# Wide projection blocks for the mixed values and the second gate in a two-layer encoder

## The chip, the cores and the metric

The kernel runs on one core of one Trainium2 chip. The metric is device time in microseconds (us) of one launch, from the first instruction to the end; the median of three runs stands for a kernel. All data are float32 in the chip's memory. The engines are PE (matrix products), ACT (activations and copies), DVE (vector work on tiles, also from PSUM), POOL (further vector work) and SP, which here only issues DMAs.

## The reference

Two layers over 2048 tokens of 1024 channels. Each layer normalises its input, projects it once into seven column ranges, and joins two kinds of mixing:

```python
SPLITS = (D_A, D_A, D_A, D_B, D_KV, D_KV, D_B)      # 512 512 512 512 128 128 512
for l in range(DEPTH):
    h = rmsnorm(x, pre_g[l])
    proj = jnp.einsum('bsd,de->bse', h, w_in[l])
    u_a, v_a, g_a, q, k, v, g_b = jnp.split(proj, idx, axis=-1)
    y_a = gmlp_group(u_a, v_a, ln_a_g[l], ln_a_b[l], spatial_w[l], spatial_b[l]) * jax.nn.silu(g_a)
    y_b = gqa_axial_attention(q, k, v, q_norm_g[l], k_norm_g[l], tables) * jax.nn.silu(g_b)
    y = jnp.concatenate([y_a, y_b], axis=-1)
    out = jnp.einsum('bse,ed->bsd', y, w_out[l])
    x = x + rmsnorm(out, post_g[l])
```

gmlp_group normalises the values v_a over their channels and mixes them across each chunk of 128 tokens with a 128x128 matrix per channel group, and adds a bias. gqa_axial_attention normalises and rotates queries (8 heads) and keys (2 heads), and attends over all 2048 tokens.

## The kernel before

*Precision.* Each float32 operand of a projection is split into a high part (hi, rounded to the matrix engine's float32 form) and a low part (lo, what is left). A projection is three passes, PASSES = ((0,0), (0,1), (1,0)), high by high, high by low and low by high, each over ND = 8 slices of 128 input channels: 24 matmuls for one tile of output.

*Tokens.* The 2048 tokens are four groups of 512 (GRP), a group is four tiles of 128 (TPG). A layer first projects everything and then attends. The projection (`run`) goes over two halves of two groups; the normalised, transposed activations of a group are two tiles `hT` (slices 0 to 3 and 4 to 7), which stay in place for all blocks of the half.

*Blocks of a half, in program order.* Weight columns come in blocks of 256 (WB). Keys and values (C_K) and the first half of the queries (C_Q) alternate by group; then the second half of the queries (C_Q+WB) for both groups; then the values of the mixing (C_VA, and C_VA+WB into the other half of the same PSUM bank) for both groups; then the gate of the attention, here called the second gate (C_GB, then C_GB+WB), each for both groups; then four blocks that join 128 columns of the first gate (C_GA) with 128 of u (C_U). In all blocks but the last four the activations are PE's stationary operand and 256 columns of weights move (`proj_tok`, out 128 tokens by 256 columns); two such tiles share one bank (`banked`). In the last four the weights are stationary and 512 tokens move (`proj_ch`). So seven of the blocks are narrow: 256 columns.

*Weights.* `load_w` (L257) brings 1 MB of raw columns by a DMA of SP; `split_w` makes hi on ACT (L267) and lo on DVE (L268) in two instructions each. Raw, hi and lo each take one slot of a pool of seven, 8 KB a partition. A load is recorded where its block is prepared and waits for its slot.

*Work behind a projection.* `do_kv` and `do_q` normalise and rotate (`norm_rope`: ACT squares, DVE reduces at L351, scales at L358, multiplies at L363 and adds at L365; POOL multiplies at L360) and hand transposes to PE for later; the results of the queries go through L411 and to memory. `do_va` takes statistics of four value tiles on DVE, scales them (L429), splits them (ACT L435, POOL L436, tile fl) and mixes: three matmuls of 256 columns per piece, read out by DVE (L448, two instructions a piece, with zbias). `do_gb` is a tanh on ACT, a product on DVE (L476) and a store. `spatial_weights` loads and transposes the mixing matrices (wsT, L233), stores their two parts and works out the bias tile zbias (L250).

*What sets the order.* PE runs in the order of the program. A list of background jobs (`bg`) is called at each `tick`, twice at most, and puts transposes and mixes between the projection's matmuls some ticks after they were asked for. The order of ACT, DVE, POOL and SP in this phase comes from a scheduler that runs before the launch; on the chip each engine takes its instructions strictly in that order. Seven PSUM banks go round among all of it (projections `pp`, transposes and mixes `pt`, maxima `pmax`). In the second half of a layer the maxima of the first attention units already run between the gate blocks.

Of the kernel before, what the change touches and what calls it, by code (L numbers as in the profile page):

```python
# [9 lines left out]
F32 = mybir.dt.float32  # L10
# [3 lines left out]
AF = mybir.ActivationFunctionType  # L14
# [5 lines left out]
P = 128  # L20
# [18 lines left out]
def encoder(ctx: ExitStack, tc, x, w_in, w_out, pre_g, post_g, ln_a_g, ln_a_b,  # L39
# [135 lines left out]
    class Project:  # L175
# [85 lines left out]
        def split_w(self, raw, n=4):  # L261
# [7 lines left out]
            return hi, lo  # L269

        def hT_jobs(self, g, tail=False):

# [41 lines left out]
        def proj_tok(self, hT, j, w, ps=None, c0=0):  # L314
            if ps is None:
                ps = ps_t("pp")
            n = 0
            for a, b in PASSES:
                for d in range(ND):
                    PE.matmul(ps[:, c0:c0 + WB], hT[d // 4][:, a, d % 4, j * P:(j + 1) * P], w[b][:, d, :],  # L320
                              start=(n == 0), stop=(n == 3 * ND - 1))
                    n += 1
                bg.tick()
            return ps

# [145 lines left out]

        def do_gb(self, g, banks, b):
            for i, ps in enumerate(banks):
                th = f_t("fa")
                nc.scalar.activation(th, ps, AF.Tanh, scale=0.5)
                nc.vector.scalar_tensor_tensor(th, th, 1.0, ps, ALU.add, ALU.mult)  # L476
                nc.sync.dma_start(gb_d[g][:, 2 * i:2 * i + 2, b * WB:(b + 1) * WB],
                                  th.rearrange("p (t e) -> p t e", t=2))

# [41 lines left out]
        def run(self, kv, first, last_jobs, first_wo):  # L521
# [5 lines left out]
            for n, gs in enumerate(halves):  # L527
# [13 lines left out]
                for i, g in enumerate(gs):  # L541
# [4 lines left out]
                    if i == len(gs) - 1:  # L546
                        raw = self.load_w([C_Q + WB])
                    self.do_kv(g, self.banked(hTs[g], w_kv))
                    if i == len(gs) - 1:
                        w_next = self.split_w(raw)  # L550
                        raw = self.load_w([C_VA])
                    self.do_q(g, self.banked(hTs[g], w), 0)
                if n == 0:
                    self.spatial_weights()
                w = w_next
                for i, g in enumerate(gs):
                    self.do_q(g, self.banked(hTs[g], w), 1)
                    if i == 0:
                        w_next = self.split_w(raw)
                w = w_next  # L560
                raw = self.load_w([C_VA + WB])
                ws = [row_t("ws", dt=F32R) for _ in range(2)]
                for i in range(2):
                    nc.sync.dma_start(ws[i].bitcast(F32), ws_d[:, i])
                w = [w, self.split_w(raw)]
                raw = self.load_w([C_GB])
                for g in gs:
                    vs = []
                    for j in range(TPG):
                        ps = self.proj_tok(hTs[g], j, w[0])  # L570
                        self.proj_tok(hTs[g], j, w[1], ps, WB)
                        v = f_t("fv")
                        nc.scalar.copy(v, ps)
                        vs.append(v)
                    self.do_va(g, vs, ws)
                w = self.split_w(raw)
                blocks = [[C_GB + WB]] + [[C_GA + c * P, C_U + c * P] for c in range(4)]
                if n + 1 < len(halves):
                    blocks.append([C_K])
                if n + 1 == len(halves):  # L580
                    self.scale_v()
                    last_jobs()
                for b in range(2):
                    raw = self.load_w(blocks.pop(0))
                    for i, g in enumerate(gs):
                        self.do_gb(g, self.banked(hTs[g], w), b)
                        if i == 0:
                            w_next = self.split_w(raw)
                    w = w_next
                for c in range(4):  # L590
# [641 lines left out]
```

## Time and profile before

| what | us |
|---|---|
| median of three runs (2775.23 to 2775.82) | 2775.79 |
| the profiled execution | 2771.47 |
| its span, first to last instruction | 2769.3 |
| PE busy in the span | 2677.1 |
| DVE busy | 1896.8 |
| ACT busy | 1522.7 |
| POOL busy | 1287.0 |

The mean clock that PE was granted was 0.992 of full speed. The rows of the profile in this text have these forms. A group of instructions: line, engine, operation, output<-inputs by their names in the program, shapes, count | busy time of the group, mean duration of one in ns | idle time of the engine just ahead of them and what ended it. A row of the timeline: start, length, engine, line, operation, count, and in brackets the idle time ahead of it with what ended it. A row of the waits: the engine and its line, what it waited for, then the total, the number of times and the longest. A row of a stretch: its start and end, its length, then busy time and count of PE, PE's weight loads, DVE, ACT and POOL, the granted clock, the busy share of the DMA engines, and GB/s.

### The profile page before, as it was taken

The numbers are of one execution on the slowest core, as the hardware profiler recorded it, in microseconds if no ns is written. First come the engines' busy times: TensorE is split into PE (matmuls) and PEld (weight loads), VectorE is DVE, ScalarE is ACT, GpSimd is POOL, SyncE is SP. The second block draws the span as 40 slices with busy tenths as digits, with TensorE's granted clock in tenths as the row PEclk, the third lists the DMA queues.
The fourth block names the chain that finished last, engine by engine and source line by source line (L and its number), as shares of the span: only waits on it lengthen the run. The fifth ranks groups of instructions, "written<-read, shape, count | busy, mean of one in ns | idle before, by whom it ended". The sixth has DMA issues, their size and how long they took to land.

```text
span 2769.3 us, 48428 instructions
## 1 busy us (share of the span) xinstructions
PE 2677.1 (97%) x18230; PEld 1782.0 (64%) x18230; DVE 1896.8 (68%) x3796; ACT 1522.7 (55%) x3005; POOL 1287.0 (46%) x1080
## 2 busy tenths in 40 slices
PE   7999999999999999999999999999999999999997
PEld 6898899764444444444589989997644444444444
DVE  8862688876666776776487528888766666666664
ACT  4221432117887787787732214221288877778774
POOL 1210122007786676776632101210277767667765
PEclk9999999999999999999999999999999999999999
DMA  4424522322222232222354334333322222221313
GB/s 143 146 81 127 165 76 81 112 63 89 89 71 81 75 98 79 82 80 80 110 179 138 115 114 134 88 92 98 94 64 72 82 70 73 81 76 47 112 46 129
DMA packets 275310, 265.31 MB, mean 96 GB/s; under 512 B 19202, under 2 KB 233346, under 8 KB 275076
## 3 DMA queue, kind: packets, MB, share of 16 engines
q1 hardware_dynamic: 275076, 262.22, 30.2%
q8 instruction: 143, 2.34, 0.3%
q14 instruction: 91, 0.75, 0.1%
HBM read 177.09 MB, written 85.07 MB: 95 GB/s over the span
## 4 chain that ended last, share of the span: by engine, by line
PE 77%; DVE 11%; ACT 5%; DMA 3%; issue 2%; POOL 1%; SPq 0%; DVEq 0%; POOLq 0%; ACTq 0%
PE pp L84 27%; PE sp L84 14%; PE po L84 11%; PE pout L84 11%; PE pmax L84 7%; PE sums L84 4%; PE pt L84 2%; DVE fc L363 2%; ACT p_parts L84 2%; ACT p_f L84 2%; DMA w_raw<-in_w_in_dram 1%; DVE mx L84 1%; DVE o_t L84 1%; DVE w_lo L268 1%; ACT w_hi L267 1%
## 5 line engine op out<-in xcount | busy, mean ns | idle before, releaser
L84 POOL TENSOR_TENSOR p_parts<-p_f,p_parts 128x512 f16<-128x512 f32 x872 | 1034.9, 1205 | 404.2 <-ACT p_f L84 304.3
L84 ACT ACTIVATE p_parts<-sp 128x512 f16<-128x512 f32 x1024 | 630.0, 615 | 296.5 <-PE sp L84 289.8
L84 DVE TENSOR_REDUCE mx<-pmax 128x1 f32<-128x512 f32 x768 | 513.0, 681 | 211.9 <-PE pmax L84 209.9
L84 PE MATMUL pout<-wo,y_t 128*128 128x512 f32 x1488 | 657.1, 506 | 0.7 <-ACT p_f L84 0.3
L84 PE MATMUL po<-p_parts,v_st 128*32 128x512 f16 (+1 forms) x3072 | 639.2, 383 | 0.2
L84 ACT ACTIVATE p_f<-sp 128x512 f32<-128x512 f32 x1024 | 632.0, 617 | 0.0
L84 PE MATMUL pp<-w_hi,hT 128*128 128x256 f32 x3584 | 502.5, 290 | 16.1 <-DVE hT L310 9.7
L84 PEld LDWEIGHTS pp<-w_hi,hT 128*128 128x128 f32 x3584 | 462.0, 194 | 21.8 <-DVE hT L310 10.9
L84 PE MATMUL sp<-q_st,k_t 128*128 128x512 f16 x1024 | 390.2, 381 | 8.3 <-DVE mx L84 5.5
L84 PE MATMUL pmax<-k_t,q_m 128*128 128x512 f16 x1024 | 389.7, 382 | 7.6 <-DVE mx L84 3.2
L84 PEld LDWEIGHTS <-v_st 128*32 128x32 f16 (+1 forms) x3072 | 193.7, 96 | 309.5 <-issue 253.0
L84 PE MATMUL sp<-q,k_t 66*128 66x512 f16 x1024 | 391.0, 382 | 0.0
L84 PEld LDWEIGHTS pout<-wo,y_t 128*128 128x128 f32 x1488 | 281.3, 190 | 128.4 <-issue 8.7
L84 PEld LDWEIGHTS <-k_t 128*128 128x128 f16 (+1 forms) x2048 | 191.5, 99 | 187.7 <-issue 74.4
L468 POOL TENSOR_TENSOR fl<-fa,fh 128x512 fp32r<-128x512 f32 x32 | 43.1, 1346 | 533.3 <-ACT fh L467 489.2
L84 PE MATMUL pp<-hT,w_hi 128*128 128x512 f32 x1024 | 271.7, 413 | 0.0
L84 PE MATMUL pp<-w_lo,hT 128*128 128x256 f32 x1792 | 262.6, 290 | 0.0
L84 PE MATMUL sums<-p_parts,one_h 128*32 128x512 f16 x2048 | 242.3, 380 | 0.0
L84 PEld LDWEIGHTS pp<-w_lo,hT 128*128 128x128 f32 x1792 | 235.5, 194 | 0.9
L84 PEld LDWEIGHTS pp<-hT,w_hi 128*128 128x128 f32 x1024 | 193.4, 190 | 35.3
L683 DVE TENSOR_REDUCE mx<-pmax 128x1 f32<-128x512 f32 x256 | 172.6, 687 | 49.1 <-PE pmax L84 47.5
L84 PEld LDWEIGHTS <-q_m 128*128 128x128 f16 x1024 | 99.8, 98 | 140.2 <-issue 42.1
(161 smaller groups left out, 2790.9 us busy)
## 6 DMA issues: line engine op xcount, KB each, us to landing
w_raw<-in_w_in_dram SPq DMA_DIRECT2D x28, 1024.0 KB
y_t<-y_d SPq DMA_DIRECT2D x56, 512.0 KB
w_raw<-in_w_in_dram SPq DMA_DIRECT2D x32, 512.0 KB
x_t<-in_x_dram SPq DMA_DIRECT2D x16, 512.0 KB
z_d<-fb SPq DMA_DIRECT2D x32, 256.0 KB
gb_d<-fa SPq DMA_DIRECT2D x32, 256.0 KB
fb<-z_d SPq DMA_DIRECT2D x32, 256.0 KB
y_d<-fh SPq DMA_DIRECT2D x32, 256.0 KB
```

What stands on the lines that cost most here:

```text
L84: return tc.keep_in_program_order(call(*args, **kw))
L267: nc.scalar.copy(hi[:, sl], raw[:, sl])
L268: nc.vector.tensor_tensor(lo[:, sl], raw[:, sl], hi.bitcast(F32)[:, sl], ALU.subtract)
L363: nc.vector.tensor_tensor(t2[:, :, :, lo:lo + 16], qn[:, :, :, hi:hi + 16], tbi[:, :, 1:2, lo:lo + 16].broadcast_to([P, 2, n, 16]), ALU.mult)
L468: nc.gpsimd.tensor_tensor(lo, th, hi.bitcast(F32), ALU.subtract)
L683: dve.tensor_reduce(s.mx[:, j, c:c + 1], ps, AX.X, ALU.max)
```

## The change

The values of the mixing and the second gate are projected in blocks of 512 columns. A wide block comes as two raws of 1 MB, each 512 columns of four slices of 128 input channels (`load_wide`), and is split into four tiles, hi and lo for slices 0 to 3 and 4 to 7 (`split_wide`); all six take slots of the same pool of seven. `proj_wide` runs the 24 matmuls of a token tile at 512 columns, with the activations stationary, and ticks after every four, so six times a tile, as the two narrow calls did together. `do_gb` now stores whole rows of a token tile. The second half of the queries moves behind the values: the order of a half is keys and first queries by group, values (wide), second queries (narrow), second gate (wide), then the four blocks of first gate and u. `spatial_weights` is called right after the first group's keys, where it came after all keys and first queries.

```diff
+        def load_wide(self, c):
+            raws = [w_t([P, ND // 2, 2 * WB], "w_raw", F32) for _ in range(2)]
+            for q, raw in enumerate(raws):
+                nc.sync.dma_start(raw, w_in[self.l, q * GRP:(q + 1) * GRP, c:c + 2 * WB]
+                                  .rearrange("(d p) e -> p d e", p=P))
+            return raws
+
+        def split_wide(self, raws):
+            parts = [], []
+            for raw in raws:
+                hi, lo = [w_t([P, ND // 2, 2 * WB], name) for name in ("w_hi", "w_lo")]
+                for d in range(0, ND // 2, 2):
+                    sl = slice(d, d + 2)
+                    nc.scalar.copy(hi[:, sl], raw[:, sl])
+                    nc.vector.tensor_tensor(lo[:, sl], raw[:, sl], hi.bitcast(F32)[:, sl], ALU.subtract)
+                parts[0].append(hi)
+                parts[1].append(lo)
+            return parts
...
+        def proj_wide(self, hT, j, w):
+            ps = ps_t("pp")
+            n = 0
+            for a, b in PASSES:
+                for d in range(ND):
+                    PE.matmul(ps, hT[d // 4][:, a, d % 4, j * P:(j + 1) * P], w[b][d // 4][:, d % 4, :],
+                              start=(n == 0), stop=(n == 3 * ND - 1))
+                    n += 1
+                    if n % 4 == 0:
+                        bg.tick()
+            return ps
...
-        def do_gb(self, g, banks, b):
-            for i, ps in enumerate(banks):
-                th = f_t("fa")
-                nc.scalar.activation(th, ps, AF.Tanh, scale=0.5)
-                nc.vector.scalar_tensor_tensor(th, th, 1.0, ps, ALU.add, ALU.mult)
-                nc.sync.dma_start(gb_d[g][:, 2 * i:2 * i + 2, b * WB:(b + 1) * WB],
-                                  th.rearrange("p (t e) -> p t e", t=2))
+        def do_gb(self, g, j, ps):
+            th = f_t("fa")
+            nc.scalar.activation(th, ps, AF.Tanh, scale=0.5)
+            nc.vector.scalar_tensor_tensor(th, th, 1.0, ps, ALU.add, ALU.mult)
+            nc.sync.dma_start(gb_d[g][:, j], th)
...
                     if i == len(gs) - 1:
-                        raw = self.load_w([C_Q + WB])
+                        raws = self.load_wide(C_VA)
                     self.do_kv(g, self.banked(hTs[g], w_kv))
+                    if n == 0 and i == 0:
+                        self.spatial_weights()
                     if i == len(gs) - 1:
-                        w_next = self.split_w(raw)
-                        raw = self.load_w([C_VA])
+                        w_next = self.split_wide(raws)
                     self.do_q(g, self.banked(hTs[g], w), 0)
-                if n == 0:
-                    self.spatial_weights()
                 w = w_next
-                for i, g in enumerate(gs):
-                    self.do_q(g, self.banked(hTs[g], w), 1)
-                    if i == 0:
-                        w_next = self.split_w(raw)
-                w = w_next
-                raw = self.load_w([C_VA + WB])
                 ws = [row_t("ws", dt=F32R) for _ in range(2)]
                 for i in range(2):
                     nc.sync.dma_start(ws[i].bitcast(F32), ws_d[:, i])
-                w = [w, self.split_w(raw)]
-                raw = self.load_w([C_GB])
-                for g in gs:
+                raw = self.load_w([C_Q + WB])
+                for i, g in enumerate(gs):
                     vs = []
                     for j in range(TPG):
-                        ps = self.proj_tok(hTs[g], j, w[0])
-                        self.proj_tok(hTs[g], j, w[1], ps, WB)
+                        ps = self.proj_wide(hTs[g], j, w)
                         v = f_t("fv")
                         nc.scalar.copy(v, ps)
                         vs.append(v)
                     self.do_va(g, vs, ws)
-                w = self.split_w(raw)
-                blocks = [[C_GB + WB]] + [[C_GA + c * P, C_U + c * P] for c in range(4)]
+                    if i == 0:
+                        w_next = self.split_w(raw)
+                w = w_next
+                raws = self.load_wide(C_GB)
+                for i, g in enumerate(gs):
+                    self.do_q(g, self.banked(hTs[g], w), 1)
+                    if i == 0:
+                        w_next = self.split_wide(raws)
+                w = w_next
+                blocks = [[C_GA + c * P, C_U + c * P] for c in range(4)]
...
-                for b in range(2):
-                    raw = self.load_w(blocks.pop(0))
-                    for i, g in enumerate(gs):
-                        self.do_gb(g, self.banked(hTs[g], w), b)
-                        if i == 0:
-                            w_next = self.split_w(raw)
-                    w = w_next
+                raw = self.load_w(blocks.pop(0))
+                for i, g in enumerate(gs):
+                    for j in range(TPG):
+                        self.do_gb(g, j, self.proj_wide(hTs[g], j, w))
+                    if i == 0:
+                        w_next = self.split_w(raw)
+                w = w_next
```

First, PE at the start of the value stage in the first half of layer 0. A row is one or several like instructions, output<-stationary and moving operands in the order of the program's names, the output's shape and a count; numbers tell tiles of one name apart. Before, a value tile begins with the last zbias matmuls (pt from wsT and sb_row) between its passes:

```order
L84 MATMUL pp_1479<-w_hi_1267,hT_145 128x256 x4
L84 MATMUL pp_1479<-w_hi_1267,hT_146 128x256 x4
L84 MATMUL pp_1479<-w_lo_1268,hT_145 128x256 x4
L84 MATMUL pp_1479<-w_lo_1268,hT_146 128x256 x4
L84 MATMUL pt_1496<-wsT_1098,fb_1107 128x256
L84 MATMUL pt_1496<-sb_row_1109,ones1_86 128x256
L84 MATMUL pp_1479<-w_hi_1267,hT_145 128x256 x4
L84 MATMUL pp_1479<-w_hi_1267,hT_146 128x256 x4
L84 MATMUL pp_1479<-w_hi_1471,hT_145 128x256 x4
L84 MATMUL pp_1479<-w_hi_1471,hT_146 128x256 x4
```

And now, at the same place:

```order
L84 MATMUL pp_1163<-w_hi_953,hT_145 128x512 x4
L84 MATMUL pp_1163<-w_hi_959,hT_146 128x512 x4
L84 MATMUL pp_1163<-w_lo_954,hT_145 128x512 x4
L84 MATMUL pp_1163<-w_lo_960,hT_146 128x512 x4
L84 MATMUL pp_1163<-w_hi_953,hT_145 128x512 x4
L84 MATMUL pp_1163<-w_hi_959,hT_146 128x512 x4
L84 MATMUL pp_1190<-w_hi_953,hT_145 128x512 x4
L84 MATMUL pp_1190<-w_hi_959,hT_146 128x512 x4
L84 MATMUL pt_1199<-ident_81,kk_947 128x128 x2
```

A tile is 24 matmuls of 512 columns where two times 24 of 256 stood, from four weight tiles, and the zbias matmuls have moved ahead of the stage.

Second, DVE at the end of the value stage of the same half, where the values of the second group are made ready. Before, their scaling (fv, L429) follows on the statistics, and the split of the weights of the first block of first gate and u (w_lo_2597) stands behind it; fb are mixes of the first group's last tile:

```order
L448 SCALAR_TENSOR_TENSOR fb_2082<-pt_2171,lng_1095,zbias_1097 64x128
L429 TENSOR_SCALAR fv_1843<-fv_1843,mv_v_2091,rs_y_2106 128x512
L429 TENSOR_SCALAR fv_1924<-fv_1924,mv_v_2091,rs_y_2106 128x512
L429 TENSOR_SCALAR fv_2005<-fv_2005,mv_v_2091,rs_y_2106 128x512
L429 TENSOR_SCALAR fv_2089<-fv_2089,mv_v_2091,rs_y_2106 128x512
L268 TENSOR_TENSOR w_lo_2597<-w_raw_2468,w_hi_2596 128x1024 x2
```

And now, with the lines of the changed program (L286 is the subtraction of `split_wide`, L481 the mix, L462 the scaling):

```order
L123 TENSOR_TENSOR rs_t_1579<-rs_y_1578 128x4
L286 TENSOR_TENSOR w_lo_1803<-w_raw_1595,w_hi_1802 128x1024
L124 SCALAR_TENSOR_TENSOR rs_t_1579<-rs_t_1579,ms_v_1564 128x4
L481 SCALAR_TENSOR_TENSOR fb_1554<-pt_1639,lng_552,zbias_554 64x128
L125 SCALAR_TENSOR_TENSOR rs_y_1578<-rs_t_1579,rs_y_1578 128x4
L481 SCALAR_TENSOR_TENSOR fb_1554<-pt_1639,lng_552,zbias_554 64x128
L123 TENSOR_TENSOR rs_t_1579<-rs_y_1578 128x4
L286 TENSOR_TENSOR w_lo_1803<-w_raw_1595,w_hi_1802 128x1024
```

The split of the second gate's second raw (w_raw_1595) now stands within the steps that lead to the scaling, ahead of all four scalings.

Third, SP's issues around that load. Before, two loads of weights of the first gate and u (w_raw) stand among the stores of mixed values (z_d) and of the gate (gb_d):

```order
L452 DMA z_d0_140<-fb_2016 512x1x128
L257 DMA w_raw_2468<-in_w_in_dram 128x8x128 x2
L452 DMA z_d0_140<-fb_2082 512x1x128
L257 DMA w_raw_2708<-in_w_in_dram 128x8x128 x2
L477 DMA gb_d0_120<-fa_2285 128x2x256
```

And now:

```order
L485 DMA z_d0_140<-fb_1455 512x1x128
L275 DMA w_raw_1595<-in_w_in_dram 128x4x512
L485 DMA z_d0_140<-fb_1508 512x1x128
L485 DMA z_d0_140<-fb_1554 512x1x128
L257 DMA w_raw_2012<-in_w_in_dram 128x8x128 x2
L373 DMA fa_1753<-in_rope_dram 128x4x128
```

The wide block's second raw stands ahead of two stores of mixed values, the weights of the first gate and u and a table of rotations (fa from rope) for the queries.

## The prediction, made before the changed kernel ran

> **What bounds the kernel now.** I read the busy shares first, then the chain that ended last, then PE's groups, and last the waits of PE in the stages that the change touches.
>
> ```profile
> PE 2677.1 (97%) x18230; PEld 1782.0 (64%) x18230; DVE 1896.8 (68%) x3796; ACT 1522.7 (55%) x3005; POOL 1287.0 (46%) x1080
> PE 77%; DVE 11%; ACT 5%; DMA 3%; issue 2%; POOL 1%; SPq 0%; DVEq 0%; POOLq 0%; ACTq 0%
> ```
>
> PE is busy for 2677.1 of 2769.3 us, and every other engine is at 68% or less: time goes only where PE issues faster or waits less. Over the whole program PE's rate counts, so the price of one matmul must be right. The groups by shape are the obvious place for it, and they mislead:
>
> ```profile
> L84 PE MATMUL pp<-w_hi,hT 128*128 128x256 f32 x3584 | 502.5, 290 | 16.1 <-DVE hT L310 9.7 <-DVE zbias L250 4.5 <-DVE k_t L396 1.2
> L84 PE MATMUL pp<-hT,w_hi 128*128 128x512 f32 x1024 | 271.7, 413 | 0.0
> ```
>
> 3584 matmuls of 290 ns would be 1039 us, yet the group was busy for 502.5: one matmul is still draining while the next runs, so the mean is no spacing. 2 x 290 - 413 = 167 ns would promise 256 us for the 1536 pairs below, which is wrong. The spacing is read from starts in stretches without a wait:
>
> ```profile
> 208.10 2.08 PE L84 MATMUL pp<-w_hi,hT 128*128 128x256 f32 x16
> 210.03 1.12 PE L84 MATMUL pp<-w_lo,hT 128*128 128x256 f32 x8
> 210.99 2.08 PE L84 MATMUL pp<-w_hi,hT 128*128 128x256 f32 x16
> ...
> 244.50 1.98 PE L84 MATMUL pp<-hT,w_lo 128*128 128x512 f32 x8
> 246.32 3.79 PE L84 MATMUL pp<-hT,w_hi 128*128 128x512 f32 x16
> 249.94 1.98 PE L84 MATMUL pp<-hT,w_lo 128*128 128x512 f32 x8
> ...
> 2743.58 4.38 PE L84 MATMUL pout<-wo,y_t 128*128 128x512 f32 x18
> 2747.79 0.62 PE L84 MATMUL pout<-wo,y_hi 128*128 128x512 f32 x2
> 2748.25 0.39 PE L84 MATMUL pout<-wo,y_lo 128*128 128x512 f32 x1
> 2748.47 0.62 PE L84 MATMUL pout<-wo,y_hi 128*128 128x512 f32 x2
> ```
>
> 256 columns: 24 from 208.10 to 210.99, 120 ns each. 512 columns with the weights stationary: 24 from 244.50 to 249.94, 227 ns each. 512 columns with the activations stationary, the roles that the changed blocks will have: 3 from 2747.79 to 2748.47, 227 ns; the 18 before them took 4.21 us, 234 ns. So doubling the columns costs 107 ns, and some 13 ns belong to each matmul whatever its width.
>
> **The change part by part.**
>
> *Wide matmuls (removes work on PE).* A narrow block takes 24 matmuls for each of 16 token tiles, 384 a layer. Four of the seven narrow blocks, two of mixed values and two of the second gate, become two wide ones: in two layers 4 x 384 x 2 = 3072 narrow matmuls become 1536 wide. Each pair gains 2 x 120 - 227 = 13.3 ns: 1536 x 13.3 = **20.5 us less**. By the 234 ns of the longer stretch a pair gains 6 ns, 9.2 us in all. I take the 227, which two stretches show, one of them with the same roles; both ends stay in the range. As many weight loads go (3072 to 1536), but they lie beside matmuls (PEld 64%) and give nothing further.
>
> The Trainium skill, "TensorE: Matmul & The Clock Gate", section "Back-to-back issue gap", speaks against the size of this: it gives the gap of isolated warm matmuls as columns/2.4 ns and 2.5 ns on top. By that a pair would gain only those 2.5 ns, 3.8 us in all as an estimate from that page. The 120 and 227 ns above disagree: the part that doesn't grow with the width is 13 ns here.
>
> *The waits of PE that move.* In the touched stages of before PE waited as follows (mixed values and second query block of the first half of layer 0 and its gates, then the same stretch of the second half):
>
> ```profile
> PE pp L84 <- DVE zbias L250: 2.5, 1, 2.5
> PE pt L84 <- POOL fl L436: 1.3, 1, 1.3
> PE pp L84 <- DVE k_t L396: 1.2, 1, 1.2
> PE pt L84 <- DVE wsT L233: 0.7, 1, 0.7
> ...
> PE pt L84 <- DVE fc L365: 3.4, 2, 3.0
> PE pmax L84 <- DVE fb L448: 0.8, 1, 0.8
> ...
> 123.23 2.05 PE L84 MATMUL pp<-w_hi,hT 128*128 128x256 f32 x8 [2.47 <-DVE zbias L250]
> 125.08 1.76 PE L84 MATMUL pp<-w_lo,hT 128*128 128x256 f32 x8
> 126.68 0.59 PE L84 MATMUL pt<-wsT,fb 128*128 128x256 f32 x2
> ...
> 372.00:402.00 30.00, 27.00 (x214) 26.63 (x214) 25.84 (x74) 9.15 (x19) 8.14 (x7) 0.94 0.27 77
> ```
>
> Layer 1 has the zbias and POOL waits again (2.0 and 1.3) and little else, so the four halves hold about 15 us. Twice a wait let the clock fall: after the 2.47 us PE took 3.45 us for 16 matmuls that take 1.92 at 120 ns (1.5 us more), and in the stretch from 372 the granted clock was 0.94 of 30 us (1.8 us more). The spatial-weight transposes and zbias move forward by one stage, into the second group's keys and queries, where DVE is as late: I keep their wait at its old size (no gain, no loss; between 0 and twice 4.5 us). The waits for fl are weighed with the weight loads below. The two falls of the clock go: -3.3. Of the waits of the query block for keys and rotations (k_t, fc, about 7.5 in all) I take half as gone, since that block now starts after two stages in which DVE catches up, and half as inherited by the wide value stage: -3.7. Together **-7.0** (between nothing and all of those 10.8).
>
> *DVE in the query block's second group (adds a wait).* There three things now meet that were apart: the mixes of the second group's values, the normalisation of the first group's queries, and the split of the next gate weights.
>
> ```profile
> L363 DVE TENSOR_TENSOR fc<-fc,fa 128x128 f32<-128x128 f32 x128 | 69.0, 598 | 10.1 <-POOL fa L342 9.2
> L358 DVE TENSOR_TENSOR fc<-pp,rs_y 128x512 f32<-128x512 f32 x32 | 21.9, 685 | 0.5
> L365 DVE TENSOR_TENSOR fc<-fc 128x512 f32<-128x512 f32 x32 | 22.4, 699 | 0.0
> L351 DVE TENSOR_REDUCE ms_q<-fb 128x8 f32<-128x512 f32 x32 | 20.6, 674 | 6.2 <-ACT fb L350 6.2
> L411 DVE TENSOR_TENSOR fl<-pt,fh 128x512 f16<-128x512 f32 x32 | 21.5, 682 | 10.9 <-ACT fh L410 10.8
> L448 DVE SCALAR_TENSOR_TENSOR fb<-pt,lng,zbias 64x128 f32<-64x128 f32 x256 | 89.3, 349 | 45.6 <-PE pt L84 42.4
> L268 DVE TENSOR_TENSOR w_lo<-w_raw,w_hi 128x1024 fp32r<-128x1024 f32 x84 | 104.4, 1256 | 18.8 <-ACT w_hi L267 17.6 <-PE pp L84 0.6
> ```
>
> Mixes of one group: 256/8 = 32 by 0.349 = 11.2 us. Normalisation of one group: 8 x 0.598 + 2 x (0.685 + 0.699 + 0.674 + 0.682) = 10.3. Split: 2 x 1.256 = 2.5. Sum 24.0 us of DVE. PE's work in that stage is 96 x 0.12 + 48 mix matmuls x 0.12 = 17.3 us. DVE falls 6.7 us behind; each mix holds a bank until DVE has read it, and seven banks in rotation absorb some of that. The wait lies between nothing and 6.7 us a half; I take 3, near the middle and near the one such wait that before shows (3.0 for fc). Four halves: **+12**, with ends 0 and 26.8.
>
> *Weight slots and loads (moves).* A wide block loads two raws and splits into four slots. For the values all four are free by the end of the keys' last stage, and DVE finishes the split before the wide stage starts: nothing. For the second gate the second raw waits for a slot that PE's last value pass holds, and DVE has its subtraction ahead of the scaling of the second group's values (the second listing of the change). Bounds for the load are two issues of before and the casts that waited for them:
>
> ```profile
> 171.51 1.29 SPq L257 DMA_DIRECT2D w_raw<-in_w_in_dram  x2
> 178.13 2.00 ACT L267 CAST w_hi<-w_raw 128x1024 fp32r<-128x1024 f32 x2 [5.82 <-DMA w_raw<-in_w_in_dram]
> 24.68 0.50 SPq L257 DMA_DIRECT2D w_raw<-in_w_in_dram  x1
> 32.28 1.05 ACT L267 CAST w_hi<-w_raw 128x1024 fp32r<-128x1024 f32 x1 [6.03 <-DMA w_raw<-in_w_in_dram]
> ```
>
> 6.0 to 7.6 us. Before has the same chain at the same place, and it set its waits for fl: the last copy of the values began at 171.72 (the stage's end), the raw of the gate came at 178.13, ACT did the two casts and only then the values' casts, POOL subtracted, and PE waited until 183.29:
>
> ```profile
> 171.72 0.59 ACT L573 COPY fv<-pp 128x512 f32<-128x512 f32 x1 [2.92 <-PE pp L84]
> ...
> 180.03 1.65 ACT L435 CAST fh<-fv 128x512 fp32r<-128x512 f32 x3
> 180.77 4.96 POOL L436 TENSOR_TENSOR fl<-fv,fh 128x512 fp32r<-128x512 f32 x3 [21.28 <-ACT fh L435]
> 183.29 0.39 PE L84 MATMUL pt<-ws,fl 128*128 128x256 f32 x1 [1.29 <-POOL fl L436]
> ```
>
> PE wanted fl there at 182.0, 10.3 us after that stage's end. Now the slot is free 12 wide matmuls (2.7 us) ahead of the end, where before issued 0.2 ahead, but DVE's two subtractions (2.5) come ahead of the values as well: the two differences cancel. I leave these waits as they are, 1.3 in two halves; the ends are 2.6 less and, with as much in all halves and the load at its 7.6, some 9 more. Behind that raw SP holds the next gate load and a rope row for POOL; the latter has some 10 us as well. The second gate's stores are as many and as large, in longer rows; DMA is not at its limit there. Attention is untouched.
>
> **Sum.** 2771.47 (the profiled execution; its span is 2769.3) - 20.5 - 7.0 + 12 = 2756.0. The median of the runs is 2775.79, 4.3 above that execution, so 2756.0 + 4.3 = 2760.3, rounded to **2760 us**, 0.6% faster.
>
> **The rivals.**
>
> *The pair doesn't gain.* If the wide matmuls run at 234 ns, as the 18 on y_t did, the gain is 9.2 instead of 20.5: 2760 + 11.3 = 2771. For it: those 18 have the same roles and a stream of weights. Against: the six behind them and the gates. The page's smaller gap (3.8 us in all) would give 2777 in the same sum. Chance 0.08.
>
> *DVE decides in the query block.* If the banks absorb nothing, PE waits 6.7 us in each half, and the clock may fall as it did after 123.23 (1.5 more): 4 x (8.2 - 3) = 21 us more, 2781; half of it 2770. For it: DVE's 24.0 us against PE's 17.3. Against: the mixes stand first in DVE's order, and before ran the same mixes beside the gate with only 1.3 us of wait. Chance 0.14.
>
> *The second gate's raw is late (the slower side).* Every us beyond about 7.6 that this load needs delays the scaling, so the mixes, by one us in each half, 4 in all. To pass before by 0.2% (2781.4) it must cost 21.4 us, 5.4 a half: a load of 13 us. For it: it stands behind z stores on the queue, in all four halves, and DVE waits for it in order. Against: neither of the two loads above took over 7.6. At 14 us the time is 2760 + 4 x 6.4 = 2786. Chance 0.08.
>
> *All waits shrink.* If DVE absorbs the query block with no wait, 12 us less: 2748. Chance 0.12.
>
> **How the numbers follow.** The forecast, 2752 to 2768, has 0.58. The measurement of this kernel can tell about 0.2%, 5.6 us, from no change: faster means below 2770.2, slower above 2781.4. Faster: 0.58 + 0.12 + 0.02 of the first rival + 0.06 of the second = 0.78. Slower: 0.05 of the late load and 0.03 of the second rival = 0.08. The rest, 0.14, is the same. The range runs from 2745, just below the case without waits, to 2777, past half of the second rival and to the top of the first; some 0.1 is left out above and 0.08 below.
>
> **What would show it.** Right: the wide groups show 24 matmuls in about 5.44 us between starts; PE's busy time falls by about 20 us; PE waits in the query block's second group for DVE (the mixes' banks) for about 3 us a half; no wait for zbias in the value stage. Wrong: wide matmuls at 234 ns or more between starts; a wait of PE for POOL's fl or a weight in the query block, of over 3 us in every half; waits in the attention that grow, since nothing there should change.

## The result and the profile after

The changed kernel takes 2798.31 us (median of 6 runs, 2797.24 to 2801.43), the kernel before 2775.51 in the same comparison: a ratio of 1.0093, interval 1.0083 to 1.0103. It is 0.9% **slower**, where 0.6% faster was forecast. The profiled execution took 2800.12 us with a span of 2798.3, 29.0 more than before.

The busy row of the page after, and the spacing of the wide matmuls in the timeline of PE, in a stretch without a wait (second gate, second group of the first half):

```profile
PE 2673.0 (96%) x16694; PEld 1697.8 (61%) x16694; DVE 1898.5 (68%) x3796; ACT 1522.7 (54%) x3005; POOL 1286.6 (46%) x1080
...
201.76 1.98 PE L84 MATMUL pp<-w_lo,hT 128*128 128x512 f32 x8
203.57 3.79 PE L84 MATMUL pp<-w_hi,hT 128*128 128x512 f32 x16
207.20 1.98 PE L84 MATMUL pp<-w_lo,hT 128*128 128x512 f32 x8
209.01 3.79 PE L84 MATMUL pp<-w_hi,hT 128*128 128x512 f32 x16
```

From 203.57 to 209.01 run 24 wide matmuls: 227 ns each, as forecast. That holds where nothing stands between them. Between the mixes four wide matmuls take from 465.01 to 465.94, 232 ns each:

```profile
465.01 1.09 PE L84 MATMUL pp<-w_hi,hT 128*128 128x512 f32 x4
465.94 0.40 PE L84 MATMUL pt<-ws,fh 128*128 128x256 f32 x2
```

PE's busy time fell by 4.1 us only, not by 20.5. A part of the difference is a lower clock: the mean granted clock of the core fell from 0.992 to 0.985. In the trace's record of it, every fall is to 0.50, in stretches of 3.4 to 13.7 us. PE was busy for 49.3 us inside such stretches, before for 26.6. If a matmul takes twice its time there, half of the 22.7 us more is lost, 11 us (an estimate, and rather high: 212 ns for 120 is seen below). So the pairs themselves took about 15 us off PE's work, not 20.5. And PE now sits idle for 2798.3 - 2673.0 = 125.3 us, where it was 92.2. The account of the 29.0 us is then: some 15 gained by the pairs, **33.1 lost in waits of PE, some 11 lost to the clock**.

Which waits these are, the waits of PE over the whole execution show (what it waited for, then total us, times, longest). Rows of before come first, then those of the changed kernel:

```profile
PE pp L84 <- DVE zbias L250: 4.5, 2, 2.5
PE pt L84 <- DVE fc L365: 3.9, 4, 3.0
PE pt L84 <- POOL fl L436: 2.6, 2, 1.3
PE pmax L84 <- DVE fb L448: 1.6, 2, 0.8
```

```profile
PE pmax L84 <- DMA q_m<-q_d: 21.4, 2, 11.1
...
PE pt L84 <- DVE fb L481: 11.0, 4, 2.8
...
PE pt L84 <- DVE fc L398: 7.3, 3, 5.0
...
PE pt L84 <- POOL fl L469: 3.6, 4, 0.9
...
PE pt L84 <- ACT fh L468: 2.2, 4, 0.5
...
PE pp L84 <- DVE zbias L250: 0.6, 1, 0.6
```

New is the first row of the changed kernel: two waits, one in the second half of each layer, for q_m, the query tile of the first attention unit whose maxima already run between the projection's matmuls. The second row is the wait that the prediction priced at 12 us. The second row stands against two waits of 0.8 for the mixes' read-outs in before (fb, L448), so 9.4 more. The wait for the queries' fc grew by 3.4 us, that for the mixes' fl and fh by 3.2, and that for zbias shrank by 3.9. Together 21.4 + 9.4 + 3.4 + 3.2 - 3.9 = 33.5; the smaller rows, some up and some down, make the remaining -0.4.

By half, the time from the first projection matmul to the first matmul of the first gate, from the starts in the traces:

| us | layer 0, first half | layer 0, second | layer 1, first | layer 1, second |
|---|---|---|---|---|
| before | 211.0 | 200.5 | 192.8 | 195.3 |
| changed | 206.3 | 222.8 | 190.6 | 210.9 |

The first halves gained 4.7 and 2.2 us; the second halves, where the maxima run and DVE reduces them, lost 22.3 and 15.6. The attention of layer 0 behind them (from the first gate on) is some 1.3 us shorter and not the place.

How q_m comes so late is read on three queues of the second half of layer 0: SP's issues, POOL, PE.

```profile
445.58 18.41 SPq L485 DMA_DIRECT2D z_d<-fb  x3
464.08 0.58 SPq L373 DMA_DIRECT2D fa<-in_rope_dram  x1
...
473.74 2.35 SPq L695 DMA_DIRECT2D q_m<-q_d  x1
...
SPq L695 <- POOL fc L393: 2.0, 1, 2.0
...
467.38 1.29 POOL L375 TENSOR_TENSOR fa<-fa,gain_q 128x512 f32<-128x512 f32 x1 [12.31 <-DMA fa<-in_rope_dram]
474.36 1.33 POOL L393 TENSOR_TENSOR fc<-fc,fa 128x512 f32<-128x512 f32 x1 [5.68 <-DVE fc L391]
...
481.43 0.61 PE L84 MATMUL pmax<-k_t,q_m 128*128 128x512 f16 x1 [11.06 <-DMA q_m<-q_d]
481.47 2.26 PE L84 MATMUL pp<-w_hi,hT 128*128 128x512 f32 x4
```

SP spent 445.58 to 464 in order on stores of mixed values, each waiting for DVE's read-outs, with the rotation table of the last query group behind them. q_m stands further back, and its tile takes over a slot from that group's normalisation, a product of POOL that ended at 475.7. Then the load took until 481.4. PE stood for 11.06 us, with the granted clock at 0.50 from 473.3 to 486.9. The maximum and the four wide matmuls that follow took 2.11 us, to 483.54, where such a step takes 1.16 later on. Before, the queries were normalised a whole value stage earlier, and q_m was issued as the second gate's stage began:

```profile
455.83 0.61 SPq L665 DMA_DIRECT2D q_m<-q_d  x1
```

### The profile page after: what moved, and what is told of

Read it like the earlier page. It is cut to its first block, busy times and chain, and to the rows that moved or that the text cites. A ratio compares the mean times of both kernels' runs of the same rounds, so it can differ in the third digit from the quotient of the medians.

```text
span 2798.3 us, 45382 instructions
## 1 busy us (share of the span) xinstructions
PE 2673.0 (96%) x16694; PEld 1697.8 (61%) x16694; DVE 1898.5 (68%) x3796; ACT 1522.7 (54%) x3005; POOL 1286.6 (46%) x1080
## 5 line engine op out<-in xcount | busy, mean ns | idle before, releaser
L84 PE MATMUL pp<-w_hi,hT 128*128 128x256 f32 (+1 forms) x2560 | 494.1, 340 | 11.0 <-DVE hT L330 9.6
L84 PEld LDWEIGHTS pp<-w_hi,hT 128*128 128x128 f32 x2560 | 394.8, 197 | 49.5 <-DVE hT L330 11.1
L84 PE MATMUL pmax<-k_t,q_m 128*128 128x512 f16 x1024 | 391.4, 383 | 26.7 <-DMA q_m<-q_d 21.4
L84 PE MATMUL pp<-w_lo,hT 128*128 128x256 f32 (+1 forms) x1280 | 248.6, 334 | 0.0
L84 PEld LDWEIGHTS pp<-w_lo,hT 128*128 128x128 f32 x1280 | 194.9, 193 | 16.7
```

The costliest lines, as they stand in the source:

```text
L84: return tc.keep_in_program_order(call(*args, **kw))
```

## The experiments

Each run is compared with runs of the kernel before on the same chip; the ratio of medians is given with its interval. Not all runs were on one chip, so two runs are best compared by their ratios. Theory: the matmuls gain what was forecast, but the order puts the second query block between the values' mixes and the first maxima, so DVE's work of three stages meets in one, and PE waits for DVE and for what is queued behind it. Rivals: the wide blocks themselves (their loads, splits, slots), or SP's queue alone.

**The query tile loaded early.** The loads of the first two q_m (`early` calls `load_qm` for units 0 and 1) are recorded ahead of the second query block:

```diff
                 raws = self.load_wide(C_GB)
+                if n + 1 == len(halves):
+                    early()
                 for i, g in enumerate(gs):
...
-                bg.add(max(n0 - 10, 0), lambda u=u: load_qm(u))
+                if u > 1:
+                    bg.add(max(n0 - 10, 0), lambda u=u: load_qm(u))
```

> The changed kernel with one edit: in the second half of each layer the query tiles (q_m) of the first two attention units are loaded ahead of the second query block instead of behind it. Theory A (q_m comes late because its slot and its place in SP's queue stand behind the normalisation of the last query group): the two waits of PE for q_m, 21.4 us together, go, and with them the lower clock behind them, some 2.7 us each: about 2798 - 27 = 2771 us. Rival B (DVE is behind at that place and q_m only hides it): PE waits there for the max reductions instead, and the time stays over 2785 us.

Measured: 2778.64 us, ratio 1.0021 (1.0012 to 1.0031), 0.72% or 20 us below the changed kernel by the two ratios. The waits for q_m are gone, and the mean granted clock rose from 0.985 to 0.989. A small part came back under another name (the second row; the first was there already, with 11.0):

```profile
PE pt L84 <- DVE fb L481: 9.6, 4, 2.8
...
PE pmax L84 <- DVE fl L444: 3.6, 2, 1.8
```

In the same place PE now waits for banks that DVE has not read yet. Theory A had 20 of its 27 us; for the rest DVE is late there too. By far the largest part of the loss is thus the place of these two loads. Whether their slot or their turn in SP's queue weighs more, this run does not tell, since it moves both.

**The order with narrow matmuls.** Wide blocks become two narrow loads, splits and calls again; order and stores stay as changed:

```diff
-                        raws = self.load_wide(C_VA)
+                        raws = [self.load_w([c]) for c in (C_VA, C_VA + WB)]
...
-                        ps = self.proj_wide(hTs[g], j, w)
+                        ps = self.proj_tok(hTs[g], j, w[0])
+                        self.proj_tok(hTs[g], j, w[1], ps, WB)
```

> The changed order and moves with the two blocks projected by narrow matmuls (two of 256 columns per slice, into the halves of one bank) and narrow weight tiles. Theory A (the wide matmul gains 13.3 ns a pair as forecast, and the order alone loses the time): 2798 + 20.5 = 2819 us, at least 2810 if slower PE work hides some of the waits. Rival B (the wide blocks, their splits and loads make the waits): near 2776 us.

Measured: 2811.22 us, ratio 1.0142 (1.0126 to 1.0158). The order, with the moved spatial weights and the stores of whole rows, costs 1.4% without any wide block, and PE waits 20.6 us for q_m and 11.0 for the mixes much as in the changed kernel: the wide blocks are not the cause, and rival B falls. But wide against narrow makes 0.49%, 13.6 us, not 20.5. By half, in the order of the table above, the wide version is 5.8 us faster, 5.8 slower, 6.7 and 2.3 faster. In the second half of layer 0 its longer waits and the lower clock behind them cost more than the pairs bring.

**The values alone wide, in the order before.**

```diff
-                        raw = self.load_w([C_VA])
+                        raws = self.load_wide(C_VA)
...
-                        w_next = self.split_w(raw)
+                        w_next = self.split_wide(raws)
...
-                        ps = self.proj_tok(hTs[g], j, w[0])
-                        self.proj_tok(hTs[g], j, w[1], ps, WB)
+                        ps = self.proj_wide(hTs[g], j, w)
```

> The kernel before in its own order, with the values alone projected by wide matmuls (768 pairs). Theory A (pairs gain 13.3 ns wherever PE is the limit): 2775.5 - 10.2 = 2765 us. Rival B (PE's time in the value stage is hidden behind DVE, or the four weight tiles of a wide block come late): 2775 us or more.

Measured: 2784.65 us, ratio 1.0042 (1.0025 to 1.0059): a miss, even the small half of the change is slower. Three halves stayed within 2 us of before, so the forecast 2.5 us a half did not show in them either, and why is open. The second half of layer 0 took 215.8 us for 200.5. The timeline of DVE and of PE there shows where they went, here with the matching row of DVE in before as the last:

```profile
370.23 0.29 DVE L212 TENSOR_SCALAR gain_k<-gain_k,g_inv 128x128 f32<-128x128 f32 x1 [4.68 <-DMA gain_k<-in_k_norm_g_dram]
370.44 2.28 DVE L519 TENSOR_REDUCE v_top<-v_st 128x1 f32<-128x2048 f32 x1
...
373.09 2.08 PE L84 MATMUL pp<-w_hi,hT 128*128 128x256 f32 x8 [5.09 <-DVE k_t L429]
...
430.66 0.29 DVE L213 TENSOR_SCALAR gain_q<-gain_q,g_exp 128x128 f32<-128x128 f32 x1 [11.49 <-DMA gain_q<-in_q_norm_g_dram]
...
433.27 1.11 PE L84 MATMUL pt<-ident,fc 128*128 128x128 f32 x4 [10.17 <-DVE fc L398]
...
422.83 0.29 DVE L213 TENSOR_SCALAR gain_q<-gain_q,g_exp 128x128 f32<-128x128 f32 x1 [0.18 <-DMA gain_q<-in_q_norm_g_dram]
```

With other tiles the scheduler placed two small steps for the next layer's gains earlier on DVE, ahead of work that PE needs. At L212 DVE stood 4.68 us for the keys' gain and at L213 11.49 us for the queries', and PE behind them 5.09 and 10.17 us: together the 15.3 us that this half lost. In before L212 waits for nothing and L213 0.18 us. So the place of two small instructions on an engine that works in order cost more than 768 pairs were to gain.

**Another order, both blocks wide.** Keys and first queries, second gate, second queries, values, first gate and u; the spatial weights go back to their old place, and further ticks ahead of each first gate finish that group's mixes (neither is shown below):

```diff
+                for i, g in enumerate(gs):
+                    for j in range(TPG):
+                        self.do_gb(g, j, self.proj_wide(hTs[g], j, w))
...
+                for i, g in enumerate(gs):
+                    self.do_q(g, self.banked(hTs[g], w), 1)
...
+                    for j in range(TPG):
+                        ps = self.proj_wide(hTs[g], j, w)
```

> Another order with both blocks wide: keys and first queries, second gate (wide), second queries (narrow), values (wide), first gate and u. The queries are then normalised beside the values, and the last maxima begin with the values; the mixes of the second value group run beside the first gate. Theory A (the loss is the query block standing between the values' mixes and the first maxima): both meetings are gone, about 2775.5 - 20.5 = 2755 us, with some 5 us either way for waits. Rival B (DVE is the limit in the second halves in any order): over 2775 us, with PE waiting for mixes or max reductions.

Measured: 2790.00 us, ratio 1.0062 (1.0047 to 1.0077). Theory A missed by 35 us: the maxima start right behind the query block here too, and PE waited for q_m again (12.4 us, two times). Its first halves, though, were shorter than before by 5.3 and 2.4 us, counted with the gates. With the early load of q_m:

> The order with the second gate first, and the first two query tiles of the maxima loaded ahead of the second query block. Theory A (there too PE waited 12.4 us for q_m and then ran at a lower clock): 2790 - 12 - 4 = 2774 us. Rival B (DVE is behind there in any case): over 2783 us.

Measured: 2781.45 us, ratio 1.0031 (1.0018 to 1.0043), 9 us less and between the two. The waits for q_m are gone, and the waits for transposes behind DVE's max reductions grew from 2.0 to 5.2 us.

**DVE relieved.** To see whether DVE is the cause, its load is cut: the rotation's partner multiplies are left out, and with them the work tile t2, in the changed kernel (with q_m early), in the kernel before, and in the changed order with narrow matmuls.

```diff
-                qn, t1, t2 = [f_t("fc").rearrange("p (t h d) -> p t h d", t=2, d=HD)[:, :, 0:n] for _ in range(3)]
+                qn, t1 = [f_t("fc").rearrange("p (t h d) -> p t h d", t=2, d=HD)[:, :, 0:n] for _ in range(2)]
...
-                for c in range(0, HD, 32):
-                    for lo, hi in ((c, c + 16), (c + 16, c)):
-                        nc.vector.tensor_tensor(t2[:, :, :, lo:lo + 16], qn[:, :, :, hi:hi + 16],
-                                                tbi[:, :, 1:2, lo:lo + 16].broadcast_to([P, 2, n, 16]), ALU.mult)
-                nc.vector.tensor_tensor(qn, t1, t2, ALU.add)
+                nc.vector.tensor_tensor(qn, t1, qn, ALU.add)
```

> The changed kernel with q_m early, and the rotation left out of queries and keys: the partner multiplies on DVE (8 of 0.6 us a query group, 8 of 0.4 us a key group, some 100 us of DVE in all) are not done, so the output is not the reference's. Theory A (PE waits because DVE is late, and each wait costs the clock behind it as well): the waits in the query block, at the start of the values and before the maxima go, some 30 us with the clock: 2778 - 30 = 2748 us, and the kernel is faster than the kernel before with the same left out. Rival B (the waits come from loads, slots and the queue of SP): at most 8 us less, 2770 us or more.

> The kernel before with the same rotation multiplies left out. Theory A: it had 15 us of waits in these stages and 3 us of lower clock, so it gains up to 18 us: 2754 to 2760 us, and the changed kernel so relieved lies below it, by 8 us or more, up to the 20.5 us of the pairs. Rival B: 2770 us, and below the changed one.

> The changed order with q_m early and the rotation multiplies left out, as in the run with the light DVE, but with narrow matmuls and narrow weight tiles for both blocks. With DVE out of the way the pairs stand alone. Theory A (13.3 ns a pair, 1536 pairs, all on the path once DVE is light): 2755 + 20.5 = 2775 us, at least 2771. Rival B (a part of the pairs lies beside waits even so, as with the loaded DVE, where wide against narrow made 13.6 us): 2768 us or less.

Measured: changed 2754.60 us, ratio 0.9930 (0.9915 to 0.9945); before 2770.65, 0.9987 (0.9977 to 0.9996); changed order narrow 2775.73, 1.0011 (1.0002 to 1.0021). DVE's busy time fell by 57 us in the changed kernel, not by the expected 100. That is worth 24 us to the changed kernel, less than the 30 of theory A but far from rival B, and some 4 us to the one before, where theory A had up to 18. In the changed kernel the waits for the mixes' banks (fb) fall from 9.6 to 1.3 us. The free tile may have helped as well; that is not separated.

The changed kernel is then 16 us faster than the one before with the same left out, but that is not all the pairs. Before gained 7.1, 2.2 and 0.8 us in three halves, and its second half of layer 0 lost 10.6 by the two gain steps seen above: DVE stood 3.16 us ahead of L212 and 13.04 ahead of L213, and PE 8.79 us in the value stage.

Wide against narrow in the same order with DVE light is the cleaner pair: 2775.73 - 2754.60 = 21.1 us (22 by the ratios), in total what theory A says. Its parts are others. The last column is an estimate that takes a matmul at clock 0.50 as twice as long:

| us | PE busy | of it at clock 0.50 | busy less half of that |
|---|---|---|---|
| before | 2677.1 | 26.6 | 2663.8 |
| changed | 2673.0 | 49.3 | 2648.4 |
| changed order, narrow | 2686.3 | 44.3 | 2664.2 |
| DVE light, q_m early, wide | 2661.2 | 20.0 | 2651.2 |
| DVE light, q_m early, narrow | 2678.4 | 25.5 | 2665.6 |

Of the 21.3 us between the profiled spans of the two light versions some 14.4 are PE's work, 2.7 the clock and 4.1 waits. All three comparisons of wide with narrow give 14 to 16 us: **the pairs are worth some 15 us, about 10 ns each**, and that the total meets the 20.5 of the forecast is partly luck.

**The normalisation put off.** In the second group of the query block DVE normalises the first group, and the mixes' read-outs stand behind it. Timeline of DVE, then of PE, in the changed kernel:

```profile
448.68 0.69 DVE L391 TENSOR_TENSOR fc<-pp,rs_y 128x512 f32<-128x512 f32 x1
449.46 2.00 DVE L396 TENSOR_TENSOR fc<-fc,fa 128x128 f32<-128x128 f32 x4
...
452.58 3.05 DVE L396 TENSOR_TENSOR fc<-fc,fa 128x128 f32<-128x128 f32 x4
455.55 0.33 DVE L481 SCALAR_TENSOR_TENSOR fb<-pt,lng,zbias 64x128 f32<-64x128 f32 x1
...
456.52 4.83 DVE L481 SCALAR_TENSOR_TENSOR fb<-pt,lng,zbias 64x128 f32<-64x128 f32 x13
...
457.02 0.77 PE L84 MATMUL pt<-ws,fh 128*128 128x256 f32 x2 [2.74 <-DVE fb L481]
457.58 0.41 PE L84 MATMUL pt<-ws,fl 128*128 128x256 f32 x1
457.80 1.91 PE L84 MATMUL pp<-w_hi,hT 128*128 128x256 f32 x8
459.50 0.63 PE L84 MATMUL pt<-ws,fh 128*128 128x256 f32 x2
```

Between 444.84 and 455.55 DVE reads out no mix, while PE makes five pieces (446.56 to 452.80), ten read-outs. With five of the seven banks so held, and the projection's tiles in others, PE waits 2.74 us for one. The 8 projection matmuls from 457.80 on take 1.70 us, 212 ns each, where 120 is their pace. DVE is not full in this stage: it is busy for 16.1 of the 20 us from 445 to 465. What holds PE up is that the read-outs stand behind the normalisation. The edit puts the normalisation off, on top of q_m early:

```diff
-                    self.do_q(g, self.banked(hTs[g], w), 1)
+                    banks = self.banked(hTs[g], w)
+                    bg.add((17, 14)[i], lambda g=g, banks=banks: self.do_q(g, banks, 1))
```

> The changed kernel with q_m early, and the normalisation of both groups of the second query block put off by 17 and 14 ticks, so that on DVE it stands behind the read-outs of the second group's mixes. Theory A (PE's wait of 2.0 to 2.8 us in the second query group comes from DVE normalising for 10 us ahead of the mixes, whose banks are then held, and the lower clock follows from it): the wait goes in all four halves, that stage falls to 15 to 16 us as in the run with the light DVE, 10 to 14 us in all: 2778 - 12 = 2766 us. Rival B (the wait only moves on, to the gate stage or the maxima): 2774 us or more.

Measured: 2781.22 us, ratio 1.0032 (1.0019 to 1.0045): no gain over q_m early alone. Both theories were half right. The wait is gone in all four halves, and that stage takes 14.8 us in each, where it took 17.0 to 19.2; the first halves come down from 207.9 and 190.9 us to 201.8 and 186.4. The second halves grow from 210.3 and 203.0 us to 213.2 and 208.2: there the wait moves into the gate stage, to the maxima:

```profile
PE pmax L84 <- DVE fa L508: 9.5, 4, 2.9
...
470.81 0.58 PE L84 MATMUL pmax<-k_t,q_m 128*128 128x512 f16 x1 [2.86 <-DVE fa L508]
472.01 2.07 PE L84 MATMUL pp<-w_hi,hT 128*128 128x512 f32 x4 [0.62 <-DVE mx L716]
```

**Each half with the order that suits it.** First the gate-first order in the first halves and the order before, narrow, in the second; then the changed order with the late normalisation in the first halves and before's in the second. Both are a branch on the half around the code shown above.

```diff
+                if n + 1 < len(halves):
...
+                else:
...
```

> First halves of both layers in the order with the second gate first and both blocks wide; second halves exactly as in the kernel before, narrow. In the profiles the first halves with that order were 5.3 and 2.4 us shorter than before, projection and gates together. Theory A (the gain is real where no maxima run): 2772 - 8 = 2764 us. Rival B (DVE carries the lateness into the second half): 2772 us or more.

> First halves in the changed order, wide, with the late normalisation; second halves as in the kernel before. Theory A: the first halves gain what the changed order gained there (4.8 and 2.2 us in the profile) and some 3.5 us each for the late normalisation: 2773 - 14 = 2759 us. Rival B (the late normalisation gives nothing, or hands its lateness on): 2766 us or more.

Measured: 2763.31 us, ratio 0.9962 (0.9947 to 0.9977), and 2756.93 us, ratio **0.9946 (0.9931 to 0.9961)**: both close to what theory A has, and the second beats the kernel before by 0.54% and the changed one by 1.5%.

**DVE's work moved to POOL.** On the first of these versions, the low parts of the weights of the second halves go to POOL:

```diff
-                        w_next = self.split_w(raw)
+                        w_next = self.split_w(raw, eng=nc.gpsimd)
```

> The version with the gate-first order in the first halves, and the low parts of the weights of the second halves' blocks subtracted on POOL instead of DVE, 12.5 us of DVE's time in each. Theory A (in the second halves DVE's load bounds the projection): some 5 us less, 2758 us. Rival B (POOL needs twice as long and delays its own products and the mixes): 2763 us or more.

Measured: 2779.36 us, ratio 1.0026 (1.0017 to 1.0036): rival B, 0.64% or some 17 us worse than without. POOL's timeline and PE's waits there:

```profile
454.20 4.77 POOL L269 TENSOR_TENSOR w_lo<-w_raw,w_hi 128x1024 fp32r<-128x1024 f32 x2 [8.74 <-PE pp L84]
...
PE pt L84 <- POOL fl L471: 10.1, 4, 2.7
```

A subtraction of 128x1024 takes 2.4 us on POOL, nearly twice DVE's 1.256, and PE waits 10.1 us for fl, the values' low part, where the version without the edit waits 4.8. That is 5.3 of the 19.6 us between the two profiled spans; PE's busy time grew by 7.9, at a mean granted clock of 0.989 for 0.993, and the rest lies in other, shorter waits.

## Why the prediction was wrong

Forecast and result lie 44.5 us apart (-15.5 against +29.0). By the account above 21.4 of them are the waits for q_m, some 14 the clock, some 6 the pairs and 6 other waits; the mixes' banks took 2.6 less than forecast.

*The step that failed, and that turned the sign: "Attention is untouched".* The term was put at nothing. But the first maxima run inside the projection's last stages, and their query tile was never followed to its slot and its place in SP's queue. The order of SP around the second gate's raw was read up to a rotation table with "some 10 us as well" and not on to q_m. That is 21.4 us of waits; the early load gave back 20 us, waits and clock together.

*The second step that failed: "The two falls of the clock go: -3.3".* It counted the falls of before and none for the waits that the change adds. The row at 123.23 showed what a wait of 2.5 us can cost, and the forecast used it in a rival only. Of the time that PE was busy at clock 0.50 in the changed kernel, 11.2 us lie behind the two waits for q_m, 15.7 behind the four for the mixes' banks, 4.5 behind that of 5.0 us for fc; about half of each is lost. The Trainium skill, "TensorE: Matmul & The Clock Gate", section "HAM oscillation — how this bites in real kernels", gives idle gaps over about 3.4 us as the bound; here 2.74 us was enough, and the measurement decides.

*The pairs: right in mechanism, mis-sized.* The 227 ns hold in runs of wide matmuls without others between them; behind mixes and maxima the next ones take 230 to 235 or more, and some 15 us are left of 20.5 (an estimate, from the table above). The sum by the formula of the Trainium skill ("TensorE: Matmul & The Clock Gate", section "Back-to-back issue gap"), an estimate of 3.8 us, is not borne out.

*DVE in the second query group: right in place, near in size, and the size partly by luck.* Forecast +12, measured 11.0 in four waits of 2.7 to 2.8, 9.4 more than before. The 3 us a half were picked between 0 and 6.7, and the 6.7 came from DVE's work against PE's. DVE was not full there; the read-outs stood behind the normalisation, where the forecast has "the mixes stand first in DVE's order".

*The waits that move: wrong by sign.* Without the clock the forecast was -3.7, all of it for keys and rotations; its "about 7.5 in all" does not come out of the rows, which show 4.6 in the stages that it names. The wait for the queries' fc grew by 3.4 instead. That for zbias, kept at its old size, fell by 3.9.

*The weight loads: nothing forecast, between -2.6 and +9; measured +3.2* (fl and fh of the mixes). The rival on the slower side, a late raw of the second gate, did not decide.

*A half as the unit.* The sum took the four halves alike, times four. They are not: in the second halves DVE also reduces the maxima, and the same edit gains in one half and loses in the other. The versions by half show it: what was had this way is the first halves' share of the pairs, with the late normalisation on top: 0.54%, some 15 us.

What stays open: whether the slot or the queue made q_m late; why the clock falls behind one wait and not behind another like it; and the second halves' placement of the next layer's gains, which cost two runs 10 to 15 us, was seen but not tried by itself.

## What to carry to other kernels

When a stage is moved, follow not only what it waits for but what now stands directly behind it: the next user of its buffer slots, and the instruction behind its stores on an in-order queue. A gain on the engine that is busiest by share counts only where no other engine is late in that stage; relieve the suspect (even by leaving work out) and measure the pair of kernels again. Even then take the clock and the remaining waits out of the difference before it is called the gain. Where stages of one kind carry different side work, choose the order for each.

## What was not expected of the hardware

A wait of PE of 2.74 us, up to 457.02, came with a granted clock of 0.50 from 456.2 to 463.0 (212 ns for a matmul of 120 ns), so the wait cost about as much again. But the price is not fixed. Behind the other three such waits of the changed kernel the clock was low for 3.4 us only, and in the changed order with narrow matmuls a wait of 2.75 us at the same place, up to 459.37, was followed by none. The rows of the two stretches, the changed kernel's first:

```profile
456.20:463.00 6.80, 5.98 (x28) 6.01 (x29) 5.11 (x15) 0.00 (x0) 0.00 (x0) 0.50 0.14 41
...
459.00:463.00 4.00, 3.63 (x30) 3.66 (x31) 3.73 (x12) 0.00 (x0) 0.00 (x0) 1.00 0.07 23
```

Over the changed kernel the waits grew by 33.1 us, and the lower clock took some 11 more.
